# Four run-time branches inside two layers replaced by one check and a loop of no or one pass at the end of the program

## The chip, the cores and the metric

One core of one Trainium2 chip. The metric is the device time of one execution of the whole program in microseconds (us); the median of several executions is compared. One further execution was taken by the hardware profiler, and all rows of a profile below come from it.

## The reference, cut to what matters

Two blocks run one after the other on 1024 tokens of width 1024. The first has two hybrid layers, the second is one layer with windowed attention and a mixture of experts. The change concerns the hybrid layers, where each query attends to the 256 keys with the highest index score:

```python
for l in range(DEPTH):                       # DEPTH = 2
    x = hybrid_layer(x, ...)                 # each calls sparse_attention(q, k, v, q_idx, k_idx, w_idx)

def block(i):                                # 8 blocks of 128 queries
    logits = einsum('bthd,bsd->bths', qib, k_idx) * IDX_DIM ** -0.5
    score = einsum('bth,bths->bts', wb, relu(logits))
    score = where(causal, score, -inf)
    _, idx = lax.top_k(score, 256)           # ties go to the lower index
    sc = where(idx <= qpos, einsum('bthd,btkd->bthk', qb, k[idx]) * scale, -inf)
    return einsum('bthk,btkd->bthd', softmax(sc), v[idx])
```

The selection has to be exact: the 256 best keys of every query row and no others.

## The kernel before, in words

Nothing is gathered. For each block of 128 queries (a tile, numbered 0 to 7) the kernel computes all scores, finds each row's threshold, and writes a mask `bias` that is 0 for a chosen key and a large negative number for the rest. Tiles 0 and 1 have at most 256 keys and use a constant causal mask. For tiles 2 to 7 `select` (two interleaved streams) computes the scores `sc`, quantises them to 16 bits (`code`), and finds a threshold by repeated counting (L606, `count`). What lies at the threshold is then resolved exactly among at most 8 candidates with MAX8 (L670 to L686). That is right as long as no row needs more than 8 values from the threshold's bucket. A flag `fl` per row and tile (L669) tells whether one does.

If a flag is set, a full search over all 32 bits of the scores (`halves`, `choose`) has to make that tile's mask anew. For it `select` stores the scores to DRAM (`scd`, L652), and `recheck` sums the flags of some tiles (a matmul against ones, L752, and two VectorE instructions, L754 and L756), loads the result into a register of VectorE and SyncE (`values_load`, L757) and opens a `tc.Switch` (L760). Its arm 1 does the full search for these tiles; its arm 0 is empty. Around the Switch three buffers of the tag `w4` are reserved (`sct` and two `wt`; the tag has four). The order is written out in each layer:

- After the second of the four column groups of z_b (`dense_T1`, f = 0 to 3, evacuated by `ev_zb`, L966 to L969) comes `recheck((2, 3, 4, 5))`.
- In the last part of the layer, when 18 of the 32 attention units are done, comes `recheck((6, 7))`.

So `recheck` is called four times in the program. Attention is a generator `attend` that is stepped between other matmuls. Unit u is one (tile, group, pair of heads). `front(u)` computes scores (L868), adds the mask and takes the maximum on VectorE (L869, which writes the buffer P, shown as Z or P), exponentiates on ScalarE (L872) and scales on GpSimd (L878). `back(u)` transposes P (L891), evacuates (L899, L900) and multiplies with the values (L904, L906, L912). A unit with at most 512 keys holds one buffer P, and until the end of the searches there are two. `heads(t)` transposes a tile's queries (L538) and evacuates them (L543, L544). A front of tile t may be issued only when t is in the set `checked`, to which `recheck` adds its tiles.

After z_b the weights `wo` of the output projection are loaded (`load_wo`, L996: 16 loads in each layer through three raw buffers, then a split on ScalarE and GpSimd, L108 and L111). Their place is that of the layer's input `hT`, so the splits begin when the last z_b matmuls are done. `fin1` and `fin2` (L1023 to L1054) are the output projection and the layer norm of a tile; they need all of `wo`.

The program's order on each engine is made at build time by a list scheduler with priorities and a simulated timeline. A Switch is one unit to it: no engine's instruction moves across it, though the scheduler chooses what is ahead of it and what is behind.

The second block ends with the experts. Its last lines (L1730 to L1735) are already of the kind that the change adds: `values_load` of a count on all five engines, and a `For_i` over overflow blocks, which makes no pass for these inputs. L1774 stands for instructions that belong to no line of the kernel's functions: branches, moves of registers, and the end of the program.

Of the kernel before, what the change touches and what calls it, by code (L numbers as in the profile page):

```python
# [10 lines left out]
FT = mybir.dt.float32  # L11
# [26 lines left out]


@with_exitstack  # L40
def tile_hybrid(ctx, tc, I, out):
    nc = tc.nc
# [516 lines left out]
    def layer(l, xin, hT=None):  # L559
# [39 lines left out]
        bias, bias_ = {}, {}  # L599
        fl = small1.tile([128, 6], BF, name="fl", bufs=1)  # L600
        scd = dram.tile([128, 6, S], FT, name=f"scd{l}")
        headed, scored = set(), set()

        def count(src, thr, op, z, junk):
            cnt = small1.tile([128, 1], FT, name=f"cnt{z}")
            V.tensor_scalar(junk[:, :src.shape[1]], src, thr, 0.0, op0=op, op1=OP.add, accum_out=cnt)  # L606
            return cnt

        def select(i):
# [12 lines left out]
            for g in range(2):  # L622
                for j in range(4):
                    h = 2 * j + g
                    for p in range(npart):
# [9 lines left out]
                        else:  # L635
                            V.scalar_tensor_tensor(d, rel[:, :w_], widx[:, i, h:h + 1], d, op0=OP.mult, op1=OP.add)  # L636
                        yield 60.0 + 1.04 * w_, False, 0.0, 2 * w_ / 2.4
            scored.add(i)


# [7 lines left out]
            G.tensor_tensor(scl, sq, mhalf[:, :1], op=OP.pow)  # L648
            G.affine_select(sc[:, n - 128:n], sc[:, n - 128:n], pattern=[[-1, 128]], compare_op=OP.is_ge,
                            fill=-BIG, base=0, channel_multiplier=1)  # L650
            A.activation(code, sc, AF.Identity, scale=scl[:, 0:1], bias=near[:, 0:1])
            nc.sync.dma_start(scd[:, i - 2, :n], sc)  # L652
            gt = bias_[i] = att.tile([128, n], BF, name=f"bias{i}")
# [14 lines left out]
            V.tensor_scalar(K2, cnt, -1.0, 256.0, op0=OP.mult, op1=OP.add)  # L668
            V.tensor_scalar(fl[:, i - 2:i - 1], K2, 8.0, None, op0=OP.is_gt)  # L669
            V.scalar_tensor_tensor(sc, gt, -1e38, sc, op0=OP.mult, op1=OP.add)  # L670
# [57 lines left out]
        def choose(sc, gt, c, cand, z, eq, pre):  # L728
# [17 lines left out]
            V.tensor_scalar(gt, gt, -1.0, BIG, op0=OP.add, op1=OP.mult)  # L746

        def recheck(tiles):

            a, b = tiles[0] - 2, tiles[-1] - 1  # L750
            pf = bank([128, 512], "sm")
            T.matmul(pf[0:1, a:b], ones, fl[:, a:b], start=True, stop=True)  # L752
            f1 = small1.tile([1, 1], FT, name="f1", bufs=1)
            V.tensor_reduce(f1, pf[0:1, a:b], axis=AX.X, op=OP.add)  # L754
            fi = small1.tile([1, 1], I32, name="fi", bufs=1)
            V.tensor_scalar(fi, f1, 0.5, None, op0=OP.is_ge)  # L756
            many = nc.values_load(fi[0:1, 0:1], engines=(DVE, SP), min_val=0, max_val=1)  # L757
            sct = tmp.tile([128, S], FT, name="sct", tag="w4", bufs=4)
            wt = [tmp.tile([128, 2, S], I16, name="wt", tag="w4", bufs=4) for _ in range(2)]
            for arm in tc.Switch({DVE: many, SP: many}, 2):  # L760
                if arm == 1:
                    for i in tiles:
                        n = 128 * (i + 1)
                        sc = sct[:, :n]
                        up, lw = wt[0][:, 0, :n], wt[0][:, 1, :n].bitcast(U16)
                        eq, pre = wt[1][:, 0, :n].bitcast(BF), wt[1][:, 1, :n].bitcast(F16)
                        nc.sync.dma_start(sc, scd[:, i - 2, :n])
                        c, cand = halves(i, sc, up, lw, bias_[i])
                        choose(sc, bias_[i], c, cand, 0, eq, pre)

# [143 lines left out]

        done, fronts, checked = [0], [0], {0, 1}

        def attend():
            while done[0] < len(units):
                u = done[0]
                while fronts[0] < len(units):  # L920
                    f = fronts[0]
                    t = units[f][0]
                    if f > u + 3 or len(free) < (1 if t < 4 else 2) or t not in checked:
                        break
                    front(f)
                    fronts[0] += 1
                    yield 200.0 + 1000.0 * (t + 1) / 4, 200.0 + 270.0 * (t + 1)
                if fronts[0] > u:
                    back(u)
                    done[0] += 1  # L930
                    yield 200.0 + 1000.0 * (t + 1) / 4, 200.0 + 270.0 * (t + 1)
                else:
                    yield 700.0
# [41 lines left out]
        for f in range(4):  # L975
            dense_T1(8, lambda k, a: hT[a][:, k, :], ev_zb(f), ZBB)
            if f == RA:
                bg_until(lambda: {4, 5} <= set(bias))
                recheck((2, 3, 4, 5))
                checked.update((2, 3, 4, 5))  # L980
        bgs.clear()
# [84 lines left out]
        while True:  # L1066
# [3 lines left out]
            bg(BGA)  # L1070
            if done[0] >= RC and 6 not in checked:
                recheck((6, 7))
                checked.update((6, 7))
            if done[0] == seen:
# [15 lines left out]
        return xout  # L1090

    ones = const.tile([128, 1], BF, name="ones")
    V.memset(ones, 1.0)
# [22 lines left out]
    x1 = layer(0, x0, hT0)  # L1116
    x2 = layer(1, x1)
    b1.close()

# [669 lines left out]
```

## Time and profile before

| | us |
|---|---|
| three executions | 2374.93, 2371.70, 2373.92 |
| median of them | 2373.92 |
| the profiled execution, its own time | 2371.94 |
| its span, first to last instruction | 2369.8 |
| TensorE matmuls busy in the span | 2140.5 |
| VectorE, ScalarE, GpSimd busy | 1521.2, 1082.8, 1082.0 |
| mean granted TensorE clock, share of full speed | 0.961 |

The profiled execution lies inside the range of the three others, and its time is 2.1 us above its span. Busy times are unions of instructions over the whole span. The stages have different limits, so the share says little about one of them.

### The profile page before, as it was taken

To read this page: it belongs to the slowest core of one execution; us is meant where nothing else is said; L and a number is where in the kernel's file an instruction comes from. 1 tells how busy PE (TensorE), PEld (TensorE's weight loads), DVE (VectorE), ACT (ScalarE), POOL (GpSimd) and SP (SyncE) were. 2 spreads that over 40 slices of the span, in tenths; PEclk is the share of its full clock that TensorE was granted. 3 is DMA by queue.
4 is the path that set the end of the run, shared out by engine and by line. 5 is a ranking of instruction groups with operands and counts; after the bars stand their busy time and mean duration, and the time that the engine had idled before them with its cause. 6 is when DMAs were issued, how large, how long until landed. Compare 5 with 4: busy or idle time off the path is not lost. (4 is left out here: it accounts for less than half of the span.)

```text
span 2369.8 us, 35974 instructions
## 1 busy us (share of the span) xinstructions
PE 2140.5 (90%) x13235; PEld 1883.9 (79%) x13235; DVE 1521.2 (64%) x3191; ACT 1082.8 (46%) x1943; POOL 1082.0 (46%) x1018
## 2 busy tenths in 40 slices
PE   5998998798989979997998999999999797999896
PEld 4898897587879979876887888888888586888785
DVE  9768887677753769685776348861010345888784
ACT  4333443554642443436554335652121222778774
POOL 4664575556736553845554345532244412222221
PEclk9999998899999989998999999999999998999998
DMA  7522112312114111223111111122121256999994
GB/s 239 188 79 86 53 32 81 106 59 68 41 47 138 45 36 49 66 67 108 68 45 41 44 41 34 30 52 67 49 67 45 98 209 200 311 325 326 317 329 116
DMA packets 146392, 260.88 MB, mean 110 GB/s; under 512 B 24681, under 2 KB 101889, under 8 KB 133905
## 3 DMA queue, kind: packets, MB, share of 16 engines
q1 hardware_dynamic: 139024, 241.59, 31.1%
q0 software_dynamic: 7168, 16.79, 3.2%
q8 instruction: 105, 1.72, 0.3%
q14 instruction: 95, 0.77, 0.1%
HBM read 228.83 MB, written 37.90 MB: 113 GB/s over the span
## 5 line engine op out<-in xcount | busy, mean ns | idle before, releaser
L111 POOL TENSOR_TENSOR wlo<-wraw,whi 128x512 fp32r<-128x512 f32 (+1 forms) x188 | 249.8, 1329 | 484.9 <-ACT whi L108 459.2
L101 PE MATMUL big<-wlo,s 128*128 128x256 f32 (+1 forms) x1536 | 440.4, 288 | 16.0 <-POOL wlo L111 16.0
L100 PE MATMUL big<-whi,s 128*128 128x256 f32 (+1 forms) x1536 | 437.8, 289 | 13.6 <-ACT s L506 8.4
L102 PE MATMUL big<-whi,s 128*128 128x256 f32 (+1 forms) x1536 | 439.6, 288 | 0.0
L101 PEld LDWEIGHTS big<-wlo,s 128*128 128x128 f32 x1536 | 301.2, 196 | 22.8 <-POOL wlo L111 19.6
L100 PEld LDWEIGHTS big<-whi,s 128*128 128x128 f32 x1536 | 298.6, 196 | 21.9 <-ACT s L506 11.0
L102 PEld LDWEIGHTS big<-whi,s 128*128 128x128 f32 x1536 | 300.6, 196 | 3.1 <-issue 0.9
L108 ACT ACTIVATE whi<-wraw 128x512 fp32r<-128x512 f32 (+1 forms) x188 | 117.7, 627 | 385.2 <-PE big L102 127.2
L111 DVE TENSOR_TENSOR ew<-s,ew 128x1024 fp32r<-128x1024 f32 x138 | 162.8, 1220 | 39.0 <-ACT ew L108 37.9
L636 DVE SCALAR_TENSOR_TENSOR s<-rel,widx,s 128x384 f32<-128x384 f32 (+3 forms) x140 | 130.6, 957 | 85.1 <-ACT rel L631 83.6
L100 PE MATMUL sm<-ew,xT 128*96 128x256 f32 x512 | 147.6, 288 | 4.8 <-ACT xT L1636 4.8
L108 ACT ACTIVATE ew<-s 128x1024 fp32r<-128x1024 f32 x138 | 137.7, 1050 | 28.6 <-PE sm L102 18.8
L102 PE MATMUL sm<-ew,xT 128*96 128x256 f32 x512 | 148.6, 290 | 1.3 <-DVE xT L1637 1.2
L101 PE MATMUL sm<-ew,xT 128*96 128x256 f32 x512 | 146.3, 286 | 0.9 <-DVE ew L111 0.9
L631 ACT ACTIVATE rel<-sm 128x384 f32<-128x384 f32 (+3 forms) x160 | 80.5, 522 | 124.1 <-PE sm L628 114.7
L100 PE MATMUL half<-s,whi 128*128 128x512 f32 x320 | 130.7, 408 | 7.1 <-ACT s L953 3.1
L101 PE MATMUL half<-s,whi 128*128 128x512 f32 x320 | 128.7, 402 | 0.0
L102 PE MATMUL half<-s,wlo 128*128 128x512 f32 x320 | 127.3, 401 | 0.0
L1674 POOL DMA_INDIRECT out_dram<-yt,ti x32 | 58.2, 1820 | 136.0 <-DMA out_dram<-yt,ti 61.0
L606 DVE TENSOR_SCALAR_CACHE_REDUCE bias<-code,cand 128x512 bf16<-128x512 int16 (+5 forms) x126 | 114.1, 924 | 0.5
L878 POOL TENSOR_SCALAR Z<-Z,rc 128x128 f32<-128x128 f32 (+7 forms) x88 | 63.9, 738 | 83.3 <-DVE rc L876 50.7
L100 PE MATMUL big<-s,whi 128*128 128x512 f32 x256 | 99.7, 390 | 0.3 <-DVE convf L1335 0.3
(618 smaller groups left out, 6014.3 us busy)
## 6 DMA issues: line engine op xcount, KB each, us to landing
wraw<-in_w_in_dram SPq DMA_DIRECT2D x164, 256.0 KB, 2.8
adaw<-in_w_ada_dram SPq DMA_DIRECT2D x48, 512.0 KB, 4.5
s<-in_w_gate_e_dram SPq DMA_DIRECT2D x23, 1024.0 KB, 9.2
s<-in_w_up_e_dram SPq DMA_DIRECT2D x23, 1024.0 KB, 11.0
s<-in_w_down_e_dram SPq DMA_DIRECT2D x23, 1024.0 KB, 11.3
X<-in_w_gate_e_dram SPq DMA_DIRECT2D x9, 1024.0 KB, 10.1
X<-in_w_up_e_dram SPq DMA_DIRECT2D x9, 1024.0 KB, 9.8
X<-in_w_down_e_dram SPq DMA_DIRECT2D x9, 1024.0 KB
```

Source lines behind the costliest of these rows:

```text
L100: T.matmul(o, lh, rh, start=start, stop=False, skip_group_check=True)
L101: T.matmul(o, lh, rl, start=False, stop=False, skip_group_check=True)
L102: T.matmul(o, ll, rh, start=False, stop=stop, skip_group_check=True)
L108: A.activation(hi, src, AF.Copy)
L111: return (sub or V).tensor_tensor(lo, src, hi.bitcast(FT), op=OP.subtract)
L606: V.tensor_scalar(junk[:, :src.shape[1]], src, thr, 0.0, op0=op, op1=OP.add, accum_out=cnt)
L631: A.activation(rel[:, :w_], ps[:, :w_], AF.Relu, scale=0.125)
L636: V.scalar_tensor_tensor(d, rel[:, :w_], widx[:, i, h:h + 1], d, op0=OP.mult, op1=OP.add)
L878: G.tensor_scalar(P[hh][:, :n], P[hh][:, :n], rc[:, hh:hh + 1], 1.0, op0=OP.mult, op1=OP.mult)
L1674: return G.indirect_dma_start(out=out, out_offset=bass.IndirectOffsetOnAxis(ap=ycol, axis=0), in_=yt, in_offset=None, bounds_check=S - 1, ...
```

## The change

The two blocks become a function that is called twice. The first call runs as before, but without `recheck`, without the stores to `scd`, and with all flags of both layers in one tile `fl` of 12 columns. At the end of its second layer the 12 columns are summed into an integer `crowd`, 0 or 1. At the very end of the program `crowd` is loaded on all engines, and a loop of `crowd` passes holds the second call: the whole computation again, in which `select` makes every mask by the full search. In the first call a front of tile t may be issued when t is below 2 or its mask has been issued.

```diff
+def tile_hybrid(tc, I, out):
+    nc = tc.nc
+    with ExitStack() as ctx:
+        crowd = ctx.enter_context(tc.tile_pool(name="crowd", bufs=1)).tile([1, 1], I32, name="crowd")
+        tile_blocks(tc, I, out, crowd)
+        more = nc.values_load(crowd[0:1, 0:1], min_val=0, max_val=1)
+        with tc.For_i(0, more, 1):
+            tile_blocks(tc, I, out)
+
 @with_exitstack
-def tile_hybrid(ctx, tc, I, out):
+def tile_blocks(ctx, tc, I, out, crowd=None):
...
-        fl = small1.tile([128, 6], BF, name="fl", bufs=1)
-        scd = dram.tile([128, 6, S], FT, name=f"scd{l}")
...
+        def mask(sc, n):
+            G.affine_select(sc[:, n - 128:n], sc[:, n - 128:n], pattern=[[-1, 128]], compare_op=OP.is_ge,
+                            fill=-BIG, base=0, channel_multiplier=1)
...
+            if crowd is None:
+                mask(sc, n)
+                gt = bias_[i] = att.tile([128, n], BF, name=f"bias{i}")
+                up, lw, eq, pre = (tmp.tile([128, n], d, name=f"bits{j}", tag="r2", bufs=6)
+                                   for j, d in enumerate((I16, U16, BF, F16)))
+                c, cand = halves(i, sc, up, lw, gt)
+                choose(sc, gt, c, cand, 0, eq, pre)
+                yield 0.0, False, 0.0, 0.0
+                bias[i] = gt
+                return
...
-            G.affine_select(sc[:, n - 128:n], sc[:, n - 128:n], pattern=[[-1, 128]], compare_op=OP.is_ge,
-                            fill=-BIG, base=0, channel_multiplier=1)
+            mask(sc, n)
             A.activation(code, sc, AF.Identity, scale=scl[:, 0:1], bias=near[:, 0:1])
-            nc.sync.dma_start(scd[:, i - 2, :n], sc)
...
-            V.tensor_scalar(fl[:, i - 2:i - 1], K2, 8.0, None, op0=OP.is_gt)
+            V.tensor_scalar(fl[:, 6 * l + i - 2:6 * l + i - 1], K2, 8.0, None, op0=OP.is_gt)
...
-        def recheck(tiles):
-            a, b = tiles[0] - 2, tiles[-1] - 1
-            pf = bank([128, 512], "sm")
-            T.matmul(pf[0:1, a:b], ones, fl[:, a:b], start=True, stop=True)
...
-            many = nc.values_load(fi[0:1, 0:1], engines=(DVE, SP), min_val=0, max_val=1)
...
-            for arm in tc.Switch({DVE: many, SP: many}, 2):
...
-                    if f > u + 3 or len(free) < (1 if t < 4 else 2) or t not in checked:
+                    if f > u + 3 or len(free) < (1 if t < 4 else 2) or t > 1 and t not in bias:
...
                 bg_until(lambda: {4, 5} <= set(bias))
-                recheck((2, 3, 4, 5))
-                checked.update((2, 3, 4, 5))
...
-            if done[0] >= RC and 6 not in checked:
-                recheck((6, 7))
-                checked.update((6, 7))
...
+    fl = small1.tile([128, 12], BF, name="fl", bufs=1)
...
     x2 = layer(1, x1)
+    if crowd is not None:
+        pf = bank([128, 512], "sm")
+        T.matmul(pf[0:1, 0:12], ones, fl, start=True, stop=True)
+        f1 = small1.tile([1, 1], FT, name="f1", bufs=1)
+        V.tensor_reduce(f1, pf[0:1, 0:12], axis=AX.X, op=OP.add)
+        V.tensor_scalar(crowd, f1, 0.5, None, op0=OP.is_ge)
     b1.close()
```

## Rows read from the trace of the kernel before

**Rows 1.** The page: the span and the engines' busy times with their share of it and the number of instructions.

```profile
span 2369.8 us, 35974 instructions
PE 2140.5 (90%) x13235; PEld 1883.9 (79%) x13235; DVE 1521.2 (64%) x3191; ACT 1082.8 (46%) x1943; POOL 1082.0 (46%) x1018
```

**Rows 2.** Busy time by stretches of the span (us from its start: then length, busy us of each engine with the number of instructions, granted clock, DMA share, GB/s). The first three lie ahead of, around and behind the first recheck of layer 0, the last around that of layer 1.

```profile
400.00:440.00 40.00, 38.41 (x186) 31.41 (x185) 35.70 (x90) 15.33 (x38) 10.50 (x14) 0.98 0.24 80
440.00:478.00 38.00, 21.84 (x90) 16.99 (x90) 19.28 (x50) 23.11 (x53) 25.91 (x26) 0.69 0.37 118
478.00:560.00 82.00, 78.34 (x443) 66.36 (x441) 59.05 (x150) 42.56 (x84) 48.67 (x39) 1.00 0.16 52
1070.00:1104.00 34.00, 21.10 (x93) 16.44 (x92) 17.71 (x49) 24.48 (x56) 25.48 (x26) 0.70 0.45 137
```

**Rows 3.** The lines of the rechecks over the whole span: register loads (L757) on the two engines, what the trace has on the full search's buffer `sct`, and the masks' last instruction (L686). Columns: line, engine, operation, times; ns min/median/max; first and last start in us.

```profile
L757 DVEq TENSOR_LOAD <-fi x4: 307/319/549, 446.0 to 1161.3; - x4
L757 SPq TENSOR_LOAD <-fi x4: 293/498/543, 446.2 to 1139.7; - x4
nothing on sct; most used: ['s', 'big', 'whi', 'sm', 'wlo', 'ew', 'half', 'tr', 'xT', 'ident', 'X', 'qT', 'Z', 'vst', 'kst', 'mx', 'hdT', 'pt', 'c', 'P', 'trx', 'pth', 'sc', 'wraw', 'kist']
L686 DVE TENSOR_SCALAR bias<-bias x12: 246/370/857, 205.9 to 1054.1; 128x512 bf16<-128x512 bf16 x2, 128x384 bf16<-128x384 bf16 x2, 128x768 bf16<-128x768 bf16 x2, 128x640 bf16<-128x640 bf16 x2
```

**Rows 4.** VectorE at the last Switch: its second branch instruction (1162 to 1163 us), and then the timeline of VectorE (start, duration, instruction, and in brackets the idle time before it and its end's cause): the first instruction behind each of the four Switches.

```profile
L1774 DVEq COMPARE_BRANCH  x1: 58/58/58, 1162.8 to 1162.8; - x1
451.66 0.68 DVE L544 TENSOR_TENSOR qT<-tr,qT 64x512 fp32r<-64x512 f32 x1 [5.55 <-ACT qT L543]
571.43 0.56 DVE L869 CUSTOM_DVE_ANT_0 P<-sc,bias 128x384 f32<-128x384 f32 x1 [3.86 <-PE sm L906]
1081.36 0.68 DVE L544 TENSOR_TENSOR qT<-tr,qT 64x512 fp32r<-64x512 f32 x1 [5.91 <-ACT s L108]
1166.80 0.69 DVE L1045 TENSOR_TENSOR s<-half,gate 128x512 f32<-128x512 f32 x1 [4.11 <-issue]
```

**Rows 5.** SyncE at three Switches. The second branch of the last one with the next transfer that was issued, and two pairs of loads of `wo` with a Switch between the two issues of a pair (start, time from the first's start to the second's end).

```profile
L1774 SPq COMPARE_BRANCH  x1: 61/61/61, 1159.3 to 1159.3; - x1
1162.89 0.34 SPq L1025 DMA_DIRECT2D rt<-xs  x1
448.40 5.69 SPq L996 DMA_DIRECT2D wraw<-in_w_out_dram  x2
1074.95 5.90 SPq L996 DMA_DIRECT2D wraw<-in_w_out_dram  x2
```

**Rows 6.** What TensorE waited for (instruction <- what ended its wait: us in total, times, longest): in 440 to 478 us (one row), in 1070 to 1104 us (two rows), in 560 to 580 us, in 1155 to 1175 us, and in 800 to 900 us (one row each).

```profile
PE sm L868 <- DVE qT L544: 3.7, 1, 3.7
PE sm L868 <- DVE qT L544: 4.0, 1, 4.0
PE tr L891 <- POOL Z L878: 3.7, 1, 3.7
PE half L100 <- DVE s L1045: 0.6, 1, 0.6
PE half L100 <- DVE s L1045: 2.6, 1, 2.6
PE tr L538 <- DVE wml L507: 9.0, 1, 9.0
```

**Rows 7.** Timelines of TensorE and VectorE: in each layer the last transposes of the unit of tile 1 that holds a buffer P, and the first VectorE instruction that writes a P for tile 2 (384 keys).

```profile
447.86 0.85 PE L891 MATMUL tr<-ident,Z 128*128 128x128 f32 x3
454.51 0.56 DVE L869 CUSTOM_DVE_ANT_0 Z<-sm,bias 128x384 f32<-128x384 f32 x1
1077.20 0.85 PE L891 MATMUL tr<-ident,Z 128*128 128x128 f32 x3
1083.24 0.56 DVE L869 CUSTOM_DVE_ANT_0 Z<-sm,bias 128x384 f32<-128x384 f32 x1 [0.47 <-issue]
```

**Rows 8.** GpSimd's timeline: the first and the last split of `wo` behind z_b in layer 0.

```profile
440.24 4.17 POOL L111 TENSOR_TENSOR s<-wraw,s 128x512 fp32r<-128x512 f32 x3 [4.51 <-ACT s L108]
472.93 1.29 POOL L111 TENSOR_TENSOR s<-wraw,s 128x512 fp32r<-128x512 f32 x1
```

**Rows 9.** The end of the program on GpSimd's sequencer, in order: the load of the loop's count (L1730), the loop's entry (L1735, 2358 to 2362 us), its closing waits (2362 us to the end), and the end of the program (L1774); then VectorE's entry of the same loop (2349 to 2352 us).

```profile
L1730 POOLq EVENT_SEMAPHORE  x5: 17/43/43, 2357.3 to 2357.6; - x5
L1730 POOLq TENSOR_LOAD <-novi x1: 501/501/501, 2357.7 to 2357.7; - x1
L1735 POOLq COMPARE_BRANCH  x2: 41/46/50, 2358.4 to 2360.1; - x2
L1735 POOLq INC_SWDGE_SEM  x1: 1464/1464/1464, 2358.6 to 2358.6; - x1
L1735 POOLq EVENT_SEMAPHORE  x10: 42/43/43, 2362.7 to 2363.5; - x10
L1774 POOLq DRAIN  x3: 46/98/5302, 2363.7 to 2369.6; - x3
L1735 DVEq EVENT_SEMAPHORE  x3: 21/21/50, 2349.8 to 2350.4; - x3
L1735 DVEq COMPARE_BRANCH  x2: 41/57/73, 2349.7 to 2350.0; - x2
```

**Rows 10.** The stores of the scores over the whole span.

```profile
L652 SPq DMA_DIRECT2D scd<-s x12: 325/338/353, 159.5 to 1000.5; - x12
```

More of the change, by code (lines that the diff above doesn't have):

```diff
@@ L746, in choose @@
             V.tensor_scalar(gt, gt, -1.0, BIG, op0=OP.add, op1=OP.mult)
-        def recheck(tiles):
-            a, b = tiles[0] - 2, tiles[-1] - 1
-            pf = bank([128, 512], "sm")
-            T.matmul(pf[0:1, a:b], ones, fl[:, a:b], start=True, stop=True)
[L753 to L756, printed above, removed]
-            many = nc.values_load(fi[0:1, 0:1], engines=(DVE, SP), min_val=0, max_val=1)
-            sct = tmp.tile([128, S], FT, name="sct", tag="w4", bufs=4)
-            wt = [tmp.tile([128, 2, S], I16, name="wt", tag="w4", bufs=4) for _ in range(2)]
-            for arm in tc.Switch({DVE: many, SP: many}, 2):
[L761 to L769, printed above, removed]
         def stream(tiles):
@@ L913, in back @@
             free.extend(taken.pop(u))
-        done, fronts, checked = [0], [0], {0, 1}
+        done, fronts = [0], [0]
         def attend():
```

## The prediction

> **What bounds the kernel now.** I began with the page. TensorE is busy for 2140.5 of 2369.8 us, VectorE for 64% [rows 1]: TensorE is the bound over the whole, so a removed wait is worth something only where TensorE stood idle because of it. The busy times by stretches show where that can be. In 400 to 440 us, with the z_b matmuls, TensorE is busy for 38.41 of 40 us; in 478 to 560 us for 78.34 of 82. Between them, in 440 to 478 us, it is busy for 21.84 of 38 us at a granted clock of 0.69, and layer 1 has the same dent, 21.10 of 34 us at 0.70 [rows 2]. The first recheck of each layer stands in these dents.
>
> A dent is not a recheck, though. In it z_b is done and the output projection cannot begin, since `wo` is still being split: the splits run from 440.24 to 474.2 us [rows 8]. TensorE has only attention, and an attention unit is a chain over four engines with two buffers P. So the views that count are TensorE's waits, and the first instruction behind each Switch.
>
> **What the Switches cost.** The arm with the full search is never taken: `sct` has no instruction in the trace [rows 3]. What remains of a recheck is a small matmul, two short VectorE instructions, a register load of 0.3 to 0.5 us on VectorE and SyncE [rows 3], and the jump over the arm. The jump is the dear part. VectorE's second branch ends at 1162.9 us and its next instruction starts at 1166.80, after 4.11 us of idleness which no producer explains ("issue") [rows 4]. SyncE's branch ends at 1159.4 and its next transfer starts at 1162.89; two loads of `wo` with a Switch between them take 5.69 and 5.90 us [rows 5], where one issue, like those of the stores, takes about 0.34 us [rows 10]. VectorE is idle for 5.55, 3.86, 5.91 and 4.11 us ahead of the instruction behind the four Switches [rows 4]: 19.4 us. Only TensorE's share of that counts:
>
> - First recheck, layer 0: TensorE waits 3.7 us for the evacuation of tile 2's queries (L544) [rows 6]. I take it whole. At least 1 us should come back, the load and branch in SyncE's and VectorE's queues. At most, the first P of tile 2 could be written as soon as a unit of tile 1 has freed its buffer: the transposes end at 448.7, the write is at 454.51 [rows 7], so 5.8 us.
> - First recheck, layer 1: 4.0 us by the same wait [rows 6]; 1 to 5.2 us (1078.05 to 1083.24) [rows 7].
> - Second rechecks: there the output projection fills TensorE, and its waits for VectorE's late L1045 are 0.6 and 2.6 us [rows 6]. I take these 3.2 us; from 0, if other matmuls would fill the gap anyway, to the 3.86 and 4.11 us of VectorE's stalls, 8.0 in all [rows 4].
> - [...] I take 1 us in each layer, an estimate; the bounds are nothing and, if the busy 21.84 and 21.10 us all ran at full clock, about 0.31 x 21.84 + 0.30 x 21.10 = 13 us.
>
> Sum of the gain: 3.7 + 4.0 + 3.2 + 2.0 = 13 us. Lower bound 2 us.
>
> **What costs or brings nothing.** The 12 stores of scores take 12 x 0.34 = 4 us of SyncE's issue time [rows 10] and their transfers; no row of TensorE's waits in rows 6 points to a load that is late behind them, so 0. If SyncE became the bound, this would be a gain of at most those 4 us. The four flag sums become one, a matmul and two VectorE instructions at the end of layer 1 beside the second block's first matmuls: 0; without that cover, under 1 us. `fl` in one tile, and the condition on `bias` in place of `checked`: all masks of tiles 2 to 5 are issued by the point where `recheck` stood, because the wait for them stays, so the generator's order hardly changes. What does change is that the scheduler may mix instructions from both sides of the old Switches.
>
> **What is added: the end.** The old end shows the price of each step for a loop of no pass. On GpSimd, the last engine, the waits ahead of the count and its load take from 2357.3 to 2358.2 us, 0.9; move, branch and fix-ups 0.3; INC_SWDGE_SEM 1.46; ten closing waits 2362.7 to 2363.6, 0.9 [rows 9]. Then comes the program's end, whose DRAIN takes 5.30 us on GpSimd [rows 9]. The new loop repeats these steps behind the old one, with nothing to hide them: the old ones lie partly under the last scatter, the new ones come after it. To be added is the jump over the body. The old loop's body is short: VectorE's entry of it has its last branch at 2350.0 and the next wait at 2350.4 [rows 9], no stall. The new body is a copy of the whole program, 35974 instructions, and the nearest row for a jump over much code is the Switch's: 1159.4 to 1162.89 on SyncE and 4.11 us on VectorE [rows 4, 5]. I take 3.7, once, as the five engines jump side by side. Sum: 0.9 + 0.3 + 1.5 + 3.7 + 0.9 = 7.3 us.
>
> [...]
>
> [...]
>
> **Sum.** -13 + 7.3 = -5.7 us on the profiled 2371.94 us, so 2366.2; that execution is 2.0 us under the median of 2373.92, so on the median's scale 2368.2, rounded 2368.
>
> **Rivals.** A measurement here cannot tell less than about 0.2%, 4.7 us, from no change.
>
> - *The gain is smaller than the end's price* (the other sign). In the dents TensorE may wait for the next thing: for GpSimd's split of `wo` and its scaling (3.7 us on POOL Z in layer 1 [rows 6]), or for one of the two buffers P. [...] It decides the sign once less than 7.3 us come back. For it: the splits last 34 us whatever the Switch does [rows 8]. Against it: the waits of 3.7 and 4.0 us end with L544, right behind the Switch [rows 4, 6].
> - *The dents close.* Without the Switch, scores of tile 2 run beside z_b, whose masks are long ready, and the two dents with 16.2 + 12.9 = 29 us of idleness [rows 2] shrink by about two thirds: -20 - 3 (second rechecks) - 2 (clock) + 7 = -18 us, 2356. For it: the first writes for tile 2 come only at 454.51 and 1083.24, behind the Switches [rows 7]. Against it: tile 1 holds both buffers P until 448.7 and 1078.0, so tile 2 could not be far ahead.
> - *The end hides under DRAIN*: -13 + 2 = -11 us, 2363. No row tells what DRAIN waits for.
> - *The new order loses by itself.* All of the order is made anew, and it holds single waits as long as 9.0 us (layer 1, evacuation of `wml`) [rows 6] that come from order alone. One more such wait eats the gain: -5.7 + 9 = +3.3 us; two +12 us, 2386.
> - *A flag is set, and the loop makes one pass*: about twice the time, 4740 us. Against it: four register loads and no full search [rows 3], with the same inputs.
>
> **How the numbers follow.** The forecast, some 0 to 10 us faster: 0.40. Gain below the end's price: 0.23. Dents close: 0.18. Hidden end: 0.09. Order loses: 0.09. One pass: 0.01. Faster by over 0.2%, below 2369.2 us: 0.22 of the forecast's share, 0.18 and 0.09, about 0.49. Within 0.2%: the remaining 0.18 of the forecast, 0.07 of the small gain and 0.02 of the lost order, 0.27. Slower: 0.16 + 0.07 + 0.01 = 0.24. The forecast alone would range from 2364 to 2374. For 8 in 10 the range has to take in the closing dents below and the second fetch or one lost wait above: 2352 to 2383.
>
> **What the profile after would show.** Right: no idle gap of about 4 us on VectorE or SyncE with "issue" behind it in the layers; busy TensorE in 440 to 478 and 1070 to 1104 us higher by some 4 us each; layer ends 5 to 7 us earlier in each layer; between the last scatter's landing and the end some 7 us more, with a gap of 3.5 to 4 us behind a branch on every engine. Wrong: a dent as deep as before with another wait in it (GpSimd's Z or `wo`); a new wait far from the old Switches, in the searches or the second block; an end that grows by 2 us or by over 10; any instruction of the full search.

## The result, and the profile after

The changed kernel takes 2387.42 us (median of six runs, 2382.26 to 2390.55), the kernel before beside it 2374.43 us: a ratio of 1.0057, 95% interval 1.0040 to 1.0073. It is slower by some 13.5 us, where the prediction said 5.7 us faster. The profiled execution took 2388.37 us, 16.4 us more than that of the kernel before. The loop made no pass.

The page after, which answers to [rows 1]:

```profile
span 2386.7 us, 35886 instructions
PE 2158.0 (90%) x13232; PEld 1885.3 (79%) x13232; DVE 1519.4 (64%) x3185; ACT 1085.2 (45%) x1943; POOL 1086.9 (46%) x1018
```

The busy times by the same stretches as in [rows 2], same columns:

```profile
400.00:440.00 40.00, 37.93 (x190) 31.16 (x188) 36.43 (x87) 16.27 (x38) 10.45 (x14) 1.00 0.18 61
440.00:478.00 38.00, 29.24 (x151) 21.58 (x151) 26.71 (x71) 23.76 (x58) 11.02 (x18) 0.91 0.26 86
478.00:560.00 82.00, 72.74 (x357) 55.63 (x357) 51.80 (x127) 41.95 (x78) 55.00 (x45) 0.94 0.24 76
1070.00:1104.00 34.00, 26.98 (x135) 20.49 (x134) 21.36 (x54) 19.34 (x47) 6.85 (x12) 0.90 0.19 67
```

The two dents, the stretches around the first rechecks, did fill: TensorE is busy for 29.24 instead of 21.84 us in 440 to 478 us, for 26.98 instead of 21.10 us around the recheck of layer 1, and the granted clock there is 0.91 and 0.90 instead of 0.69 and 0.70. But the stretch behind the first dent, which was full (78.34 of 82 us at 1.00), now holds 72.74 us at 0.94. Layer 0 ends later: the first VectorE instruction on layer 1's index weights (`widx`) starts at 722.55 us, before at 715.94, 6.6 us later; by 1370 us the whole program is 10.9 us behind. What is late stands in SyncE's queue. Its issues of the 16 loads of `wo`, in layer 0 and in layer 1 (times; ns min/median/max; first and last start), after and then before:

```profile
L993 SPq DMA_DIRECT2D wraw<-in_w_out_dram x16: 327/328/425, 469.2 to 499.4; - x16
L993 SPq DMA_DIRECT2D wraw<-in_w_out_dram x16: 327/328/427, 1106.5 to 1136.6; - x16
...
L996 SPq DMA_DIRECT2D wraw<-in_w_out_dram x16: 327/333/627, 413.2 to 467.5; - x16
L996 SPq DMA_DIRECT2D wraw<-in_w_out_dram x16: 327/330/383, 1045.7 to 1097.1; - x16
```

In layer 0 the first is 56 us late, the last 32. What SyncE waited for (instruction, what ended the wait: us in total, times, longest), in 440 to 480 us and then, last line, in 1070 to 1112 us:

```profile
SPq L291 <- DVE pt L899: 18.8, 1, 18.8
SPq L993 <- DVE ptl L899: 3.6, 1, 3.6
...
SPq L1022 <- DVE pt L899: 24.2, 3, 21.1
```

The load of `scale1` (L291) stands 18.8 us at the head of SyncE's queue for a place of ring `w4` (a ring is a fixed number of buffers that are handed out in turn, `w4` with four, `wraw` with three), in layer 1 a load of `rt` (L1022) for 21.1 us; all loads of `wo` are behind them, and the second of them then waits 3.6 us more for a place of `wraw` that a unit of attention holds as its `pth` (the high half of its transposed P; `ptl` is the low half). GpSimd's splits, first and last of layer 0 ([rows 8]: 440.24 and 472.93), and the first instruction of the output projection on VectorE, 3.5 us later than before's 488.74:

```profile
474.49 1.29 POOL L123 TENSOR_TENSOR s<-wraw,s 128x512 fp32r<-128x512 f32 x1 [2.12 <-ACT s L120]
501.95 2.52 POOL L123 TENSOR_TENSOR s<-wraw,s 128x512 fp32r<-128x512 f32 x2 [0.68 <-ACT s L120]
...
492.26 0.69 DVE L1042 TENSOR_TENSOR s<-half,gate 128x512 f32<-128x512 f32 x1 [8.14 <-PE half L114]
```

Last the end of the program on GpSimd's sequencer, answering to [rows 9]: the load of the sum, INC_SWDGE_SEM (an instruction that the entry of the old loop has too), the branch over the body, the first wait behind it, and the program's DRAIN:

```profile
L47 POOLq TENSOR_LOAD <-crowd x1: 305/305/305, 2373.9 to 2373.9; - x1
L48 POOLq INC_SWDGE_SEM  x1: 1435/1435/1435, 2374.9 to 2374.9; - x1
L48 POOLq COMPARE_BRANCH  x1: 33/33/33, 2376.4 to 2376.4; - x1
L48 POOLq EVENT_SEMAPHORE  x12: 42/43/43, 2379.3 to 2380.3; - x12
L1775 POOLq DRAIN  x3: 46/98/5302, 2380.5 to 2386.4; - x3
```

From the old loop's last branch at 2373.7 to the DRAIN at 2380.5 this is 6.8 us, with 2.9 us of it behind the branch at 2376.4.

### The profile page after: what moved, and what is told of

Its sections match the earlier page's. It is cut to its first block, busy times and chain, and to the rows that moved or that the text cites. A ratio compares the mean times of both kernels' runs of the same rounds, so it can differ in the third digit from the quotient of the medians.

```text
span 2386.7 us, 35886 instructions
## 1 busy us (share of the span) xinstructions
PE 2158.0 (90%) x13232; PEld 1885.3 (79%) x13232; DVE 1519.4 (64%) x3185; ACT 1085.2 (45%) x1943; POOL 1086.9 (46%) x1018
## 5 line engine op out<-in xcount | busy, mean ns | idle before, releaser
L112 PEld LDWEIGHTS big<-whi,s 128*128 128x128 f32 x1536 | 295.6, 194 | 20.7 <-ACT s L518 9.3
L114 PEld LDWEIGHTS big<-whi,s 128*128 128x128 f32 x1536 | 297.5, 194 | 3.5 <-issue 0.9
L877 POOL TENSOR_SCALAR Z<-Z,rc 128x128 f32<-128x128 f32 (+7 forms) x96 | 69.4, 736 | 135.7 <-DVE rc L875 94.4
L871 ACT ACTIVATE Z<-Z,mx 128x128 f32<-128x128 f32 (+7 forms) x96 | 67.3, 702 | 89.6 <-DVE mx L868 88.8
```

The costliest lines, as they stand in the source:

```text
L112: T.matmul(o, lh, rh, start=start, stop=False, skip_group_check=True)
L114: T.matmul(o, ll, rh, start=False, stop=stop, skip_group_check=True)
L871: e = A.activation(Pv, Pv, AF.Exp, bias=mx[:, npart - 1:npart], scale=-1.0, accum_out=sm[:, hh:hh + 1])
L877: G.tensor_scalar(P[hh][:, :n], P[hh][:, :n], rc[:, hh:hh + 1], 1.0, op0=OP.mult, op1=OP.mult)
```

## The experiments

They were run in batches beside the kernel before; each ratio is to that. 0.001 is 2.4 us. The intervals are some 0.0015 wide to either side, so a difference between two kernels is sure to about 5 us, and I lean on those that several pairs show. Each trace is one execution: that of e5 took 5 us more than its kernel's median, those of e4 and e14 11 us more. So landmarks (the start of one and the same instruction in two traces) that differ by a few microseconds say little by themselves.

**e1, no end.** The last three lines of `tile_hybrid` (load of the sum, loop, second copy) are gone.

> The changed kernel without its end: the flags are summed and compared as before, but nothing loads the result, and the loop with the second copy of all blocks is left out (so nothing would be repeated if a flag stood). If the end costs what the sum of the prediction says and what the last transfer of the two traces shows (7.3 to 7.7 us), the time is 7.5 us under the changed kernel, some 2380 us or 1.0025 of the kernel before, and the layers are still later than before by the 5 us that remain. Rival: all of the loss is the end; then it comes out at 1.000 or below. Rival: the end hides; then it stays at 1.0055.

1.0028 (1.0014 to 1.0042). The end is worth 0.0029, 7 us; the other half of the loss is in the layers.

**e2, SyncE's order pinned.**

```
+            with tc.issue_after(wod[0].ins):   # last load of w_out
                 d = nc.sync.dma_start(rt, xin[t * 128:(t + 1) * 128, :])
```

and `mod_row(scale1, 1, 1)` likewise.

> The changed kernel with one order pinned: on SyncE's queue the loads of scale1 and rt stand behind the last of the sixteen loads of w_out, as in the kernel before; the places of the ring wraw are still taken by the attention's pth of one unit traced ahead of them. Theory A (what holds w_out back is the head of SyncE's queue, scale1 and rt waiting for a place of ring w4): both layers come back, the gain of 13 us shows, and the time is 1.0055 less some 20 us: 2367 us or 0.997. Theory B (it is the two places of wraw, which that unit holds until its transposes are evicted): the loads of w_out stand behind those places all the same, the splits move by less than 5 us, and the time stays at 1.004 to 1.006. Theory C (the attention that runs ahead loses by itself, w_out is only late with it): stays at 1.0055 even where w_out's splits are early.

1.0102 (1.0082 to 1.0121), worse than the changed kernel. The loads of `wo` stand first now, and it does not help. SyncE's issues in layer 0, and then its longest wait in 440 to 480 us:

```profile
L995 SPq DMA_DIRECT2D wraw<-in_w_out_dram x16: 327/328/426, 442.3 to 498.8; - x16
```

```profile
SPq L995 <- DVE ptl L899: 29.8, 1, 29.8
```

The first goes at 442.3 us, and the second stands 29.8 us for a place of `wraw` until `pth` has been read. Theory A, which was my first reading of the waits above, falls: the head of the queue was only what one saw. Theory B, the places of `wraw`, has the wait and the splits right (the first starts at 473.41 us, in the changed kernel at 474.49) and the time wrong: it put this kernel at 1.004 to 1.006. Why the pinned order costs more stays open.

**e3, one constant.** `SD` is the number of finished units from which a unit may keep its `pth` and `ptl` in the rings `wraw` and `wlo`. The generator's counters tell where the places go. In the kernel before, 12 units of attention have been traced when the last column group of z_b ends; in the changed kernel 13, an odd number. The line `while done[0] % 2: next(att_)` then traces one more unit, number 13 (counted from 0), ahead of `load_wo`; no background work is left at that point (the second condition for these rings) and 13 is past `SD`, so its two `pth` take two of the three places of `wraw`, in front of the 16 loads.

```
-    SD, WOE = 12, 17
+    SD, WOE = 14, 17
```

> The changed kernel with one constant changed, SD from 12 to 14: the one unit of attention (number 13) that the changed condition lets the program trace between the last Z block and the loads of w_out keeps its pth and ptl in ring w4 instead of wraw and wlo. All loads of w_out can then go ahead of it, and on SyncE's queue they stand ahead of scale1 and rt again. Theory B (the places of wraw in trace order): splits of w_out back at 440 to 473 us in layer 0 and 1071 to 1102 in layer 1, the stalls of the Switches gone as well, so the 13 us of the prediction arrive and only the end of 7.5 us stands against them: some 2368 us, 0.9975 of the kernel before. Theory A expects the same here. Theory C (attention ahead of the output projection loses by itself): no better than the changed kernel, 1.0055.

1.0009 (0.9996 to 1.0023): 0.0048, 11 us, come back by one constant, and SyncE's order righted itself. Its issues in both layers, and the first dent (columns of [rows 2]):

```profile
L993 SPq DMA_DIRECT2D wraw<-in_w_out_dram x16: 327/328/344, 411.6 to 463.5; - x16
L993 SPq DMA_DIRECT2D wraw<-in_w_out_dram x16: 327/328/531, 1048.2 to 1099.5; - x16
```

```profile
440.00:480.00 40.00, 29.20 (x136) 21.08 (x137) 24.66 (x64) 29.40 (x68) 27.98 (x31) 0.84 0.39 124
```

So the places of `wraw`, in the order in which the program is traced, are what held `wo`. But 0.9975 was expected; the Switches' 13 us did not arrive here either.

**e4, old layers with the new end.** Both rechecks put back into the changed kernel.

> The layers of the kernel before (both Switches in each layer, stores of the scores, the old condition) with the end of the changed kernel behind them: flags of all thresholds summed again and the loop over the second copy. All theories that put the end at 7.5 us expect 1.003 of the kernel before (2382 us) and layers that match it within 1 us; if the size of the program with its second copy costs something in the layers too, the layers are later than before from the first Switch on, and the time is above 1.005.

1.0020 (1.0006 to 1.0034); the layers' landmarks are 2 to 5 us behind those of the kernel before, where 1 us was expected. This is the trace that took 11 us more than the median, so it neither shows nor excludes a cost of the longer program in the layers. The end by itself: some 5 us.

**e5, only the Switches gone.**

```
-                    if f > u + 3 or len(free) < (1 if t < 4 else 2) or t > 1 and t not in bias:
+                    if f > u + 3 or len(free) < (1 if t < 4 else 2) or t not in checked:
...
                 bg_until(lambda: {4, 5} <= set(bias))
+                checked.update((2, 3, 4, 5))
```

and no end (the condition stands in the first copy alone).

> The changed kernel without its end (no load of the result, no loop) and with the old condition for the attention of tiles 2 to 7 put back: a set that is filled at the two places where the rechecks stood, with no Switch there. So the program is traced in the order of the kernel before, and only the branches, the loads of fi and the stores of the scores are gone (nothing would be repeated if a flag stood). If the four Switches cost what the prediction's sum says, 13 us, the time is 0.9945 of the kernel before. If most of that gain is taken back by the next wait, as e3 less the end suggests (1.0009 less 0.0029), it is 0.998, some 5 us. Nothing at all, 1.000, would say that the Switches were hidden.

0.9989 (0.9974 to 1.0004): 2.6 us, not 13. The dents of layer 0 and layer 1 in the kernel before, and then in this kernel:

```profile
440.00:480.00 40.00, 23.84 (x102) 18.53 (x102) 20.36 (x53) 25.09 (x59) 26.60 (x28) 0.70 0.40 126
1070.00:1110.00 40.00, 26.88 (x127) 20.88 (x126) 22.64 (x63) 30.24 (x69) 26.84 (x28) 0.74 0.49 153
...
440.00:480.00 40.00, 25.20 (x108) 19.67 (x107) 19.04 (x50) 26.36 (x59) 27.38 (x28) 0.67 0.42 132
1070.00:1110.00 40.00, 27.55 (x123) 21.49 (x122) 19.96 (x51) 27.25 (x61) 26.86 (x28) 0.73 0.47 149
```

The dents are there without the Switches: 1.4 and 0.7 us of idleness came back in them, where the prediction took 3.7 and 4.0. Why, for layer 0, is in the timelines of ScalarE around the evacuation of tile 2's queries: first the kernel before, then e5, and e5's VectorE:

```profile
450.46 0.63 ACT L108 ACTIVATE s<-wraw 128x512 fp32r<-128x512 f32 x1 [4.03 <-DMA wraw<-in_w_out_dram]
451.00 0.57 ACT L543 ACTIVATE qT<-tr 64x512 fp32r<-64x512 f32 x1
```

```profile
450.51 0.63 ACT L117 ACTIVATE s<-wraw 128x512 fp32r<-128x512 f32 x1 [2.67 <-DMA wraw<-in_w_out_dram]
451.04 0.57 ACT L552 ACTIVATE qT<-tr 64x512 fp32r<-64x512 f32 x1
...
451.65 0.68 DVE L553 TENSOR_TENSOR qT<-tr,qT 64x512 fp32r<-64x512 f32 x1 [4.78 <-ACT qT L552]
```

In both, ScalarE stands 4.03 and 2.67 us before a split of `wo` whose transfer has not landed; the evacuation of the queries is behind it and starts at 451.00 and 451.04; VectorE's half follows at 451.66 [rows 4] and 451.65. SyncE issued that load of the kernel before at 447.10, ahead of its Switch, though right behind its load of `fi` (446.2 to 447.0), so a little of this wait is the recheck's own; e5 issues it at 446.87.

The Switch ran beside this wait and ended with it. VectorE's second branch starts at 447.6 in the kernel before; in e13 below the same branch starts at 449.2, and the next instruction, with no producer that explains its wait ("issue"), at 453.29, 4.0 us behind the branch's end. The same 4.0 us would end at 451.7 here, where 451.66 is measured:

```profile
L1774 DVEq COMPARE_BRANCH  x1: 73/73/73, 447.6 to 447.6; - x1
...
L1774 DVEq COMPARE_BRANCH  x1: 73/73/73, 449.2 to 449.2; - x1
```

Two waits end together there, and to take one away leaves the other.

The scheduler also makes its order anew without the Switches: e5's first output projection reaches VectorE at 495.09 us, 6.4 us later than before's 488.74, while TensorE waits for no more than 1.2 us in 478 to 500 us. So the 2.6 us are the Switches less what the new order costs. TensorE's idle time gives the same size by itself: from the start to the last output projection of layer 1 it is 143.7 us in the kernel before and 141.7 in e4, which has the Switches, and 138.7 and 138.9 in e5 and e12, which have none: 3 to 5 us less. (Busy time in this stretch is 1157.5 us in the kernel before and 1163.9 in e4 with the same layers; it differs that much from one execution to the next.) The stretches of the kernel before, e4, e5 and e12:

```profile
0.00:1301.15 1301.15, 1157.49 (x7502) 1036.84 (x7502) 954.88 (x2140) 589.75 (x1107) 737.29 (x685) 0.95 0.26 79
0.00:1305.66 1305.66, 1163.92 (x7503) 1044.12 (x7503) 951.17 (x2143) 590.84 (x1107) 737.75 (x685) 0.95 0.26 79
0.00:1303.44 1303.44, 1164.75 (x7499) 1044.22 (x7499) 948.47 (x2135) 590.79 (x1107) 738.50 (x685) 0.95 0.25 76
0.00:1301.06 1301.06, 1162.20 (x7499) 1040.63 (x7499) 951.03 (x2135) 590.45 (x1107) 738.83 (x685) 0.95 0.25 76
```

**e6, e3 without its end.**

> e3 without its end: new condition, SD at 14, no load of the result and no loop. Additive costs would give e3 less the end, 1.0009 less 0.0029: 0.998. It stands beside e5 for what the new condition is worth once the ring wraw is free: if attention that starts earlier helps, it is below e5 by 2 us or more; if it is the order of before that is good, above it.

0.9970 (0.9955 to 0.9985), 4.5 us under e5. This points to a gain from attention that starts earlier once `wo` is on time; the pair with the end, e3 and e12, goes the same way by 2.6 us. Neither is beyond what two kernels can be told apart by.

**e7, the loss put into the kernel before.**

```
-        while done[0] % 2:
+        while done[0] < 14:
             next(att_)
```

> The kernel before with one edit: two units of attention (12 and 13) are traced ahead of the loads of w_out, as the changed kernel comes to do by its condition; Switches, stores and end stay as they are. Unit 13 then takes two places of wraw ahead of them. Theory B (those places): both layers lose what the changed kernel's layers lost beyond the gain of the Switches, 8 to 12 us in all, 1.004 to 1.005. Rival (the loss needs the missing Switches, attention that runs ahead): no change, 1.000 to 1.001.

1.0108 (1.0087 to 1.0130), 26 us: the same mechanism with Switches, old condition and old end, two to three times as dear as expected. Here unit 12 takes places of `wraw` as well, and each layer loses 12 us by the landmarks.

**e8, second Switches alone.** e5 with `recheck((6, 7))` put back.

> e5 with the second recheck of each layer (tiles 6 and 7) put back as in the kernel before, with its Switch and the stores of the scores; the first one of each layer stays out, and so does the end. The prediction puts the two second Switches at 3.2 us: then this is 0.0013 above e5. If the second ones carry all that e5 gains, it is at 1.000; if they are hidden, it equals e5.

1.0029 (1.0016 to 1.0043), 0.0040 above e5, three times the forecast, and above the kernel before, which has both pairs. The landmarks place it in layer 1: 5.0 us behind the kernel before at the last z_b evacuation, 12.2 at the first output projection, 11.9 at the last, where e5 goes from 3.7 to 7.5 and back to 2.3. So against e5 it is 1.3, 4.7 and 9.6 us behind: about half is there ahead of the second Switch, by another order, and the other half comes from the Switch on. How single Switches are priced apart from the order stays open.

**e9 and e10, most of `wo` not loaded.** In `load_wo` only the first three blocks are loaded; the splits read `kept[k % 3]`.

> The kernel before, its Switches in place, with 13 of the 16 loads of w_out left out in each layer: three blocks are loaded, and all 16 splits read one of them (so the output projection multiplies by wrong weights). Neither ScalarE's nor GpSimd's splits wait for a transfer any more in the stretches around the first rechecks, and no load of w_out stands behind a Switch in SyncE's queue. It is half of a pair with e10. If the transfers of w_out are what TensorE's dent really hangs on, this alone is faster than the kernel before by 2 to 6 us; if the Switches hold TensorE as the prediction says, it is at 0.999 to 1.000.

> e5 (no Switches, no end, the old condition) with the same 13 loads of w_out left out in each layer. Theory: in e5 the loads of w_out, for which ScalarE's splits wait ahead of the evacuation of tile 2's queries, took the place of the Switch; without them the Switches' whole price shows, and e10 is 8 to 13 us below e9. Rival: the Switches cost some 3 us whatever stands beside them; e10 is 1 to 4 us below e9, as e5 is below the kernel before.

1.0178 and 1.0150, and neither can be used as meant: the wrong weights change the routing (both make a pass of the overflow loop), and GpSimd, free to run its splits back to back, lets attention wait. TensorE's longest wait in 440 to 480 us, in e9 and in e10:

```profile
PE tr L891 <- POOL Z L878: 14.7, 1, 14.7
```

```profile
PE tr L887 <- POOL Z L874: 17.0, 1, 17.0
```

The scaling of P is queued behind the splits. Take `wo`'s transfer away, and GpSimd is the next wait. The question of the pair, what the Switches cost without that transfer, is not answered by it.

**e11, a conditional block in place of the loop.** `with tc.If(more > 0):` on e3.

> e3 (SD at 14, everything else as changed) with the loop of no or one pass written as a conditional block: the same test of the same sum, and the same second copy. The far jump stays (2.96 us from GpSimd's last branch to its next wait in the changed kernel); INC_SWDGE_SEM (1.44 us) and the re-arming of the semaphores should go, and perhaps the closing waits (1.05 us). Then it is 1.5 to 3 us below e3, 0.9995 to 1.0003 of the kernel before; equal to e3 if a conditional block closes as dearly as a loop.

0.9989 (0.9976 to 1.0003). In the traces its end takes 5.6 us where e3's takes 6.7: the closing waits are gone, INC_SWDGE_SEM is not (1.45 us). By time it is 4.7 us under e3; the end shows 1.1 of that, and the rest is within what two kernels can be told apart by.

**e12, the condition alone undone**, with the end.

> The changed kernel with one part undone: the old condition for the attention of tiles 2 to 7 (a set filled where the rechecks stood), all else as changed, the end too. If the parts add, it is e5 plus the end: 0.9989 + 0.0029 = 1.0018, so the new condition is worth 9 us of the changed kernel's loss. If the condition does no harm by itself, 1.0055.

1.0020 (1.0008 to 1.0033). The new condition costs 0.0037 with the end (e12 to the changed kernel) and 0.0039 without (e5 to e1): 9 us.

**e13, e14 and e15, ScalarE out of that step.**

```
-            A.activation(q[hi], ps[hi], AF.Copy)
+            V.tensor_copy(q[hi], ps[hi]) if vec else A.activation(q[hi], ps[hi], AF.Copy)   # vec: tiles 2, 3
```

> The kernel before with one step moved: for tiles 2 and 3 VectorE, not ScalarE, copies the high half of the transposed queries out of PSUM, so ScalarE's splits, which wait for transfers of w_out, no longer stand ahead of it. VectorE then does it right behind its Switch. Theory (wo's transfer on ScalarE held the step in layer 0, not the Switch): the first qT of tile 2 is written some 1 us earlier than 451.66, then bounded by the Switch's jump; time 0.999 to 1.001.

> e5 (no Switches, no end, the old condition) with the same step moved to VectorE for tiles 2 and 3. Nothing holds VectorE there now, so the first qT of tile 2 in layer 0 is written as soon as its transposes are done, near 449 us, 2 to 2.5 us ahead of e5 and of the kernel before. If ScalarE's wait had taken the Switch's place for good, e14 is 3 us or more below e5 (0.9976 or less); if the chain simply waits next for GpSimd's scaling, its time is that of e5, 0.9989.

> e11 (SD at 14, conditional block at the end) with the same step moved to VectorE. A whole kernel with nothing left out. If ScalarE's wait matters, below e11: 0.997; if GpSimd is next, as e11, 0.9989.

1.0045 (1.0027 to 1.0063), 1.0023 (1.0009 to 1.0038) and 0.9990 (0.9975 to 1.0005). The first two miss what was expected: with the step on VectorE the kernel is 8 us slower without Switches (e14 against e5) and 11 with them (e13 against the kernel before), while on e11 the same move costs nothing (e15); the cause is open. e13 less e14 is 0.0022, 5 us, so here too the Switches are worth less than 13. With ScalarE out of the way the Switch does become the bound, in e13 on VectorE; in e14 the wait for the queries is gone from the list, and ScalarE's evacuation of P's transposes has its place (below VectorE's row of e13, then of e14 TensorE's longest wait in 436 to 482 us and the dent):

```profile
453.29 0.68 DVE L544 TENSOR_TENSOR qT<-tr,qT 64x512 fp32r<-64x512 f32 x1 [5.08 <-issue]
```

```profile
PE sm L900 <- ACT pt L895: 4.7, 2, 3.6
```

```profile
440.00:480.00 40.00, 23.27 (x97) 17.92 (x96) 20.14 (x49) 20.92 (x48) 25.88 (x26) 0.70 0.38 116
```

TensorE's idle time in 440 to 480 us is 16.2 us in the kernel before, 14.8 in e5, 16.4 in e13 and 16.7 in e14: nearly the same, whichever wait is taken away. e15 gains nothing over e11. No whole kernel tried here is surely faster than the kernel before; e11 and e15, some 2.5 us under it, are the best.

## Why the prediction was wrong, step by step

The loss has three parts: the end 7 us (e1; 5 to 9 in e4, e12 less e5, and e3 less e6), the new condition 9 us (the changed kernel less e12; e1 less e5), the Switches with the order that goes with them -2.6 us (e5). Taken along one chain, from the kernel before by e5 and e1 to the changed one, they sum to the 13.5 us measured by construction. That they add is shown by e12, the end without the condition: 1.0018 expected from the parts, 1.0020 measured. In the prediction's terms, two steps failed: the gain of 13 us, of which 2.6 came, and the term 0 for the new condition, which cost 9 us.

- **The end: right.** 7.3 us forecast, 6.8 in the trace, 5 to 9 by the pairs. Its terms: load and waits ahead of it 0.5 instead of 0.9, moves and fix-ups 0.7 instead of 0.3, INC_SWDGE_SEM 1.44, closing waits 1.0, the far jump 2.9 instead of 3.7 us on GpSimd. The old loop's branch, over a short body, is followed after 0.2 us. Why one takes 2.9 us and the other 0.2, no run shows. Nor does a run show the "second fetch" that the range's upper end takes in: GpSimd's branch at the end of the new loop stands at 2380.4 us, and the DRAIN follows at 2380.5. DRAIN takes 5.30 us before and after: it hides nothing, and that rival falls.
- **First rechecks, 3.7 and 4.0 us "by the same wait": wrong in layer 0, mostly in layer 1.** The failed step is to have followed the wait to VectorE's instruction and stopped there because a Switch stood ahead of it. [rows 4] names the releaser of 451.66: `ACT qT L543`, not "issue". One step further back stands ScalarE's wait for a transfer of `wo`, which ended together with the Switch. In layer 1 the queries were ready on ScalarE at 1078.0 and VectorE took them at 1081.36, so the Switch did hold it there. In e5 the transposes of these queries begin at 1079.92, before at 1076.35, behind a wait of 4.3 us for GpSimd's scaling (3.7 before), and VectorE's step falls at 1083.01: 3.6 us behind the kernel before has become 1.7, and the rest of the 4.0 us was taken by the next waits. So 1.4 and 0.7 us of idleness came back in the two dents; e5's are the "dent as deep as before with another wait in it" that the prediction named as a sign of being wrong. The price of the jump was about right (3.7 us taken; 4.0 behind e13's branch, of 5.08 us idle), its place on the path was not.
- **Clock, 2.0 us: wrong with it.** No run shows the 1 us that was taken for each layer; in its place e5 has a granted clock of 0.67 in 440 to 480 us, before 0.70. In the changed kernel it is higher in the dents (0.91 and 0.90) and lower behind the first one (0.94 in 478 to 560 us, before 1.00).
- **Second rechecks, 3.2 us: borne out in layer 1's idle time, not settled in the whole.** TensorE is busy for 36.38 of 40 us around layer 1's second Switch in the kernel before, and for 39.75 in e5, so 3.4 us of idleness went; in layer 0 nothing did (37.24 and 36.94 us in 560 to 600). Put back in e8, the pair costs some 9 us, only half of it from the Switch on. The stretch in the kernel before, then in e5:

```profile
1150.00:1190.00 40.00, 36.38 (x199) 30.69 (x198) 29.02 (x68) 20.62 (x37) 22.82 (x18) 1.00 0.27 94
1152.00:1192.00 40.00, 39.75 (x225) 34.36 (x224) 33.16 (x72) 21.27 (x39) 24.45 (x19) 1.00 0.25 86
```

- **"The condition on `bias` in place of `checked`: the generator's order hardly changes", 0: wrong, and 9 us.** The argument looked at which masks exist when `recheck` is passed. But the old condition also kept tile 2 back until the second column group of z_b was through; without it one more unit is traced by the end of the four groups, the parity step adds another, and two places of a ring of three are given away ahead of 16 loads (e3, e7). In the diff this is one term of one line.
- **The rivals.** "The gain is smaller than the end's price" was right about the gain, and near the mechanism it named (the next wait in the dent: for GpSimd's split of `wo` and its scaling; in layer 0 it was ScalarE's split of `wo`): alone it gives 0.9989 + 0.0029 = 1.0018, which e12 confirms. "The new order loses by itself" was right too; that its price, 9 us, was taken from a wait elsewhere (layer 1's `wml`) makes the figure luck. Each was given a tenth to a quarter; both happened, and the measured 2387 us lies 4 us above the range's end. "The dents close" happened in the trace (21.84 to 29.24 us) and was given back in 478 to 560 us, where the output projection waited for the splits of `wo` (the row below; in the kernel before there is no such wait in 478 to 530 us).

```profile
PE half L113 <- POOL s L123: 5.0, 6, 2.3
```

## What to carry to other kernels

When a wait ends just behind a suspect, follow it through the engine that the row names until an instruction has no releaser or a transfer stands there. Two waits can end together, as near 451.7 us in layer 0 here, and then a stall is worth only what is left when its neighbour's wait is taken as it is. In a kernel whose order comes out of a generator, a changed condition is a changed order: count, before and after, what is traced ahead of each ring's next user, since a ring gives its places in that order and a queue that issues in order passes one late place on to everything behind it (in e2 the second load of `wo` stood 29.8 us, and the last of the 16 went at 498.8 us, before at 467.5). A loop of no pass at the very end is not free: here 7 us with nothing beside it, 2.9 of them the jump over its long body.

## What was not expected of the hardware

- A jump over the long body took 2.9 us on GpSimd at the end (2.5 to 2.9 on ScalarE, SyncE and VectorE), and over the arm of a Switch 4.0 us on VectorE in e13; over the old loop's short body 0.2 us on GpSimd.
- GpSimd's DRAIN takes 5.30 us in the kernel before, behind the old loop, and in the changed one, behind the 6.8 us of the new end.
- The conditional block of e11, which is not taken, has INC_SWDGE_SEM too (1.45 us).
